# Hybrid mLSTM and sliding-window attention layer: softmax denominators through a ones column, first-head q and k kept outside the attention pool, gate rows turned later, and a front that turns x by transposes alone

## The chip, the cores and the metric

The kernel runs on one core of a Trainium2 chip. The metric is the device time of one execution in microseconds, taken as the median of the runs. Engines are named as in the profile: PE (matrix multiply), PEld (its weight loads), DVE (vector), ACT (scalar), POOL (GpSimd) and SP (the engine that issues most DMAs).

## The reference, cut to what matters

One layer on x of 1024 positions by 1024 features, all in float32:

```python
h = rms_norm(x, pre_mix_g) * (1 + sc1) + sh1          # sc1, sh1 from c @ w_ada
proj = h @ w_in                                        # q,k,v,o of 4 mLSTM heads, gates, q,k,v of attention
qk_ml = silu(causal_dwconv(qk_ml, ml_conv_w, ml_conv_b))     # 4 taps
logf = log_sigmoid(gates[..., ML_H:] + ml_f_b)
h_ml = mlstm_chunkwise(q_ml, k_ml, v_ml, i_pre, logf)  # stabilised by running maxima
...
# attention: 8 heads, 2 kv heads, window 128, blocks of 128
s = where(band, q @ k.T / 8, -inf);  m = maximum(max(s), sink)
p = exp(s - m);  denom = sum(p) + exp(sink - m);  o = (p / denom) @ v
...
x = x + g1 * rms_norm(concat(h_ml, o_at) @ w_out)
x = x + g2 * rms_norm(conv_ffn(norm(x)))               # up 1024 -> 2x2816, conv, gated gelu, down
```

## The kernel before

Every large product is a split one: each float32 operand is cut into a high and a low part (`hi`, `lo`), and `mm3` (L87) issues three matmuls for it. The work runs in stages, named here with the times at which the trace shows them.

**Front, 0 to 33 us** (it overlaps the first products). It is ordered by hand. Eight blocks of x (128 rows each) are loaded. `x_square` sums their squares on ACT, POOL makes `rst` of them, and `x_turn` (L262) turns each block so that features lie on the partitions: the first four are multiplied by `rst` on DVE (L265) and turned by eight PE transposes (L274), the last four are turned by matmuls with the diagonal matrix `dg` of `rst` (L268, L276). `x_evac` (L279) copies the turned halves to `xT` on ACT or DVE. Matmuls named `cb` spread the conditioning vector c over the partitions, and `ada_sum` (L166) multiplies it on DVE with the 48 pieces of w_ada, one 128x1024 operation each; pieces 0, 1, 8, 9 and so on are due here, the rest is spread through the later stages by `ada_bg`.

**Keys and values, 26 to 92 us**: the product for attention's k and v, then `kv_evac` (L467): rope, a copy of v to `vat` (L471), the difference `vdf` of v in this block and the one before (L473), transposes of k, and its split `khi`, `klo`. v and gates of the mLSTM heads follow.

**Attention, 112 to 236 us.** `att_group` runs twice over eight blocks of 128 queries, with four heads each (groups 0 and 1). In a block, `token_group` computes q (`tg`, L88 to L90), then `att_front` (L487) turns it, multiplies with this block's and the last block's keys (`s`, L515), and merges the two parts into one 128x128 tile per head, `sm`: the current block on and below the diagonal, the last block above it (L523, L524). DVE takes the maximum (L525) and `ngm` (L526); ACT exponentiates and sums each row (L528, `accum_out`); DVE adds the sink's term (L531) and inverts (L532). `att_back` (L535) transposes the probabilities on PE (`pt`, L538) and copies them to `pT` (L541). POOL selects the current block's part into `pN` (L545). PE multiplies (`po`, L551): pT with the last block's v, plus pN with `vdf`. DVE scales with `den` into `mix` (L554, two operations). Group 1 also squares the result on ACT (`asq`, L562). One or two ada pieces go to DVE in each block.

**Gates.** Between the two groups' code stands the chain that turns the gates of the mLSTM heads into rows (`pg`, L622 to L624), makes prefix sums and maxima of them in nearly thirty small DVE operations, stores `urow` in DRAM (`u_dram`, L657), exponentiates, and turns the results back into columns with `pg2` (L664 to L671), copied to `gcol`.

**mLSTM q and k, 186 to 340 us.** `conv_chunk` (L682) runs for q0, k0, q1, k1 to q3, k3. For each it computes the product (`cvq`, `cvk`; L88 to L90) in two halves of 512, copies them to `ub` on ACT (L692: one tile `ubq` for all q, one tile `ubk` for all k), and runs the convolution: one ACT operation and three DVE operations on a tile `cy` (L696, L698), a tanh on ACT into `z` (L699), and the product of both on DVE (L700). The tiles `cy` and `z` lie in the pool `lp`, which is opened after attention's pool `ap_` and that of the keys, `kp`, are released (L677 to L679), so the first convolution cannot start before attention's last read. `ml_head` (L703 on) loads row sums from `u_dram` into `U`, makes decay matrices `dm` on POOL and ACT (L717 to L719), weights k on DVE (`kw`, L733), and runs over eight chunks (`mS`, `st`, `tot`, L743 and around).

Then the o projection (330 to 395 us), w_out, the FFN's up product (500 to 924) and down product (924 to the end).

Except for the front, no order is written out. The framework's scheduler orders each engine's queue by its own timeline from the program's dependencies, and the number of buffers of a tile name sets when a writer waits for readers: two PSUM buffers for all of tg and cv (`mm`), and pools pA, pB, pC for s, pq/pt/xtp and po/pg.

## Time and profile before

| | us |
|---|---|
| median of 3 runs | 1156.37 (1156.13 to 1157.1) |
| the profiled execution | 1158.24 |
| its span, first to last instruction | 1156.1 |
| PE busy | 1121.0 (97%) |
| DVE busy | 859.9 (74%) |
| ACT busy | 572.0 (49%) |
| POOL busy | 189.7 (16%) |
| mean granted PE clock | 0.987 |

The profiled execution lies 1.87 us above the median; all sums are made against it and then carried over to the median. Busy time is what an engine spent in its own operations, whatever it waited for between them. A wait row names the instruction that waited, the one that released it, the total, the times and the longest wait. In a table of windows each entry is a busy time with the number of instructions in brackets, then the granted clock as a share of full speed, the share of the DMA engines and their GB/s. A timeline row gives start, duration, engine, line, output and inputs, and in square brackets the engine's idle time ahead of it and what ended that.

### The profile page before, as it was taken

The page shows a single profiled execution, that of the slowest core. Times are in us where ns is not written, and L with a number is a line of the kernel's source. Part 1 is how long each engine was busy: PE and PEld are TensorE (multiplying, and loading weights), DVE is VectorE, ACT ScalarE, POOL GpSimd, SP SyncE. Part 2 cuts the span into 40 slices and gives each one's busy share as a digit, 9 for nine tenths or more (in the row PEclk, how much of TensorE's full clock was granted, in tenths as well). Part 3 has the DMA queues.
Part 4 walks back from the last instruction along what each step waited for, and adds up shares of the span by engine and source line. Part 5 has one row for each costly group of instructions (what it writes and reads, how often), then busy time and mean ns, then how long its engine had stood idle before and what let it go on. Part 6 is the DMA issues. An engine that isn't in the chain of part 4 may idle for free.

```text
span 1156.1 us, 16247 instructions
## 1 busy us (share of the span) xinstructions
PE 1121.0 (97%) x5951; PEld 947.0 (82%) x5951; DVE 859.9 (74%) x1523; ACT 572.0 (49%) x1177; POOL 189.7 (16%) x244
## 2 busy tenths in 40 slices
PE   7999998988989999999999999999999999999997
PEld 6999997877879988877788888888888888787885
DVE  5945879478885446788897797879787874787666
ACT  6642545534444545476455454545454554345452
POOL 2022327373575400000000000000000000000021
PEclk8999998989999999999999999999999999999999
DMA  9622335151110521333332333133313468553545
GB/s 359 227 88 75 109 113 188 48 200 56 37 56 20 164 74 73 110 109 110 119 118 62 112 119 119 55 118 119 119 55 110 136 200 276 170 173 119 173 116 202
DMA packets 54464, 144.74 MB, mean 125 GB/s; under 512 B 5304, under 2 KB 5616, under 8 KB 54384
## 3 DMA queue, kind: packets, MB, share of 16 engines
q1 hardware_dynamic: 52496, 138.19, 36.0%
q10 hardware_dynamic: 1888, 5.51, 1.2%
q8 instruction: 47, 0.77, 0.3%
q14 instruction: 33, 0.27, 0.1%
HBM read 115.09 MB, written 28.60 MB: 124 GB/s over the span
## 4 chain that ended last, share of the span: by engine, by line
PE 64%; DVE 7%; POOL 3%; DMA 2%; issue 2%; ACT 2%; SPq 0%; POOLq 0%; DVEq 0%; ACTq 0%
PE X L1009 7%; PE X L1008 7%; PE X L1007 7%; PE Y L1009 4%; PE Y L1007 4%; PE Y L1008 4%; PE y L90 3%; PE y L88 3%; PE y L89 3%; DMA rb<-in_w_down_dram 2%; PE Z L1009 1%; DVE cyk L698 1%; PE Z L1007 1%; PE Z L1008 1%; PE dx L1180 1%
## 5 line engine op out<-in xcount | busy, mean ns | idle before, releaser
L93 POOL TENSOR_SCALAR rsb<-ssb 128x1 f32<-128x1 f32 x4 | 2.3, 584 | 613.0 <-ACT junk L1232 612.8
L166 DVE SCALAR_TENSOR_TENSOR ada<-ada,cb 128x1024 f32<-128x1024 f32 x48 | 61.4, 1284 | 1.5 <-DMA ada<-in_w_ada_dram 1.5
L1007 PE MATMUL X<-S,wl 128*128 128x512 f32 x156 | 62.4, 400 | 0.0
L1009 PE MATMUL X<-S,wl 128*128 128x512 f32 x156 | 61.9, 396 | 0.0
L1008 PE MATMUL X<-S,wl 128*128 128x512 f32 x156 | 61.7, 395 | 0.0
L1017 DVE SCALAR_TENSOR_TENSOR yg<-ug,cv,yg 128x1023 f32<-128x1023 f32 (+1 forms) x44 | 56.3, 1280 | 5.8 <-ACT yg L1014 5.7
L85 ACT CAST wl<-T 128x512 fp32r<-128x512 f32 x41 | 25.5, 622 | 65.5 <-PE X L1008 61.7
L1017 DVE SCALAR_TENSOR_TENSOR yv<-uv,cv,yv 128x1023 f32<-128x1023 f32 (+1 forms) x44 | 56.2, 1278 | 1.9 <-ACT yv L1014 1.9
L85 ACT CAST w<-T 128x512 fp32r<-128x512 f32 x47 | 29.1, 623 | 40.3 <-PE Z L1009 34.7
L85 DVE TENSOR_TENSOR A<-ra,A 128x512 fp32r<-128x512 f32 x46 | 31.6, 688 | 17.3 <-ACT A L85 17.2
L1061 DVE TENSOR_TENSOR uv<-q,X 128x512 f32<-128x512 f32 x22 | 15.1, 686 | 38.5 <-PE X L1009 38.5
L85 ACT CAST A<-ra 128x512 fp32r<-128x512 f32 x46 | 28.5, 620 | 30.3 <-PE dxu L1181 14.1
L85 DVE TENSOR_TENSOR w<-T,w 128x512 fp32r<-128x512 f32 x47 | 32.1, 686 | 14.8 <-ACT w L85 14.8
L85 ACT CAST B<-rb 128x512 fp32r<-128x512 f32 x44 | 27.2, 619 | 29.9 <-DMA rb<-in_w_down_dram 12.5
L85 DVE TENSOR_TENSOR B<-rb,B 128x512 fp32r<-128x512 f32 x44 | 30.2, 688 | 9.2 <-ACT B L85 8.6
L1009 PE MATMUL Y<-S,wl 128*128 128x512 f32 x92 | 36.4, 396 | 0.0
L1007 PE MATMUL Y<-S,wl 128*128 128x512 f32 x92 | 36.4, 395 | 0.0
L1008 PE MATMUL Y<-S,wl 128*128 128x512 f32 x92 | 36.2, 394 | 0.0
L85 ACT CAST wl<-fu 128x512 fp32r<-128x512 f32 x21 | 13.0, 620 | 46.7 <-PE Y L1008 43.5
L1008 PEld LDWEIGHTS X<-S,wl 128*128 128x128 f32 x156 | 29.3, 188 | 7.6 <-issue 0.5
L1007 PEld LDWEIGHTS X<-S,wl 128*128 128x128 f32 x156 | 29.3, 188 | 7.5 <-issue 0.5
L1009 PEld LDWEIGHTS X<-S,wl 128*128 128x128 f32 x156 | 29.3, 188 | 7.0
(621 smaller groups left out, 4027.6 us busy)
## 6 DMA issues: line engine op xcount, KB each, us to landing
ada<-in_w_ada_dram SPq DMA_DIRECT2D x48, 512.0 KB, 4.4
ra<-a_dram SPq DMA_DIRECT2D x30, 512.0 KB, 3.8
fu<-in_w_up_dram SPq DMA_DIRECT2D x26, 512.0 KB, 3.5
a_dram<-yg SPq DMA_DIRECT2D x22, 512.0 KB, 3.7
rb<-in_w_down_dram SPq DMA_DIRECT2D x44, 256.0 KB, 3.6
fu_False<-in_w_up_dram SPq DMA_DIRECT2D x18, 512.0 KB, 3.5
a_dram<-s SPq DMA_DIRECT2D x11, 512.0 KB, 5.1
x<-in_x_dram SPq DMA_DIRECT2D x8, 512.0 KB, 6.5
```

The lines of the kernel that those rows point to most:

```text
L85: return A.copy(hi, src), eng.tensor_tensor(lo, src, f(hi), op=ALU.subtract)
L88: T.matmul(ps, lh, rh, start=first, stop=False)
L89: T.matmul(ps, lh, rl, start=False, stop=False)
L90: T.matmul(ps, ll, rh, start=False, stop=last)
L166: return V.scalar_tensor_tensor(w, w, 0.5, cb, op0=ALU.mult, op1=ALU.mult, accum_out=mod[:, j : j + 1])
L698: V.scalar_tensor_tensor(y, ub[:, 1 + i : 1 + i + S], w(i), y, op0=ALU.mult, op1=ALU.add)
L1007: T.matmul(ps, w[:, 0, ks], a[:, 0, k, :], start=st, stop=False, skip_group_check=True)
L1008: T.matmul(ps, w[:, 0, ks], a[:, 1, k, :], start=False, stop=False, skip_group_check=True)
L1009: ends = T.matmul(ps, w[:, 1, ks], a[:, 0, k, :], start=False, stop=en, skip_group_check=True)
L1017: V.scalar_tensor_tensor(t[:, sh:], src[:, : S - sh], w(tap), t[:, sh:], op0=ALU.mult, op1=ALU.add)
L1061: V.tensor_tensor(uv[:, 512:], p5, px_, op=ALU.add)
L1180: T.matmul(ps[tb], a[:, 0, ts], w[:, 1], start=False, stop=False, skip_group_check=True)
```

## The change

**Attention.** `vat` gets a column of ones behind each kv head's 64 values, written once. `vdf` and its subtraction go. The selection on POOL is now done twice in each block but the first of a group: `pN` is the current part, and `pT` is then cut in place to the last block's part. The exponentials no longer write row sums: the 65th column of `po` holds the sum of probabilities, and `att_back` adds it to the sink's term, inverts and scales all four heads by one DVE operation.

**Pools.** `khi` and `klo` move into attention's pool. A pool `first_qk`, opened ahead of attention, holds one tile `yq`, one `yk` for heads 0 and 2 (heads 1 and 3 have theirs in `lp`). The tanh is written over `ub` and the product over `y`, so `z` and `cy` go; `ub` now stays in use until the last product has read it. Heads 1 and 3 have a `ubk` of their own for k.

**Gates.** The chain's scratch lies in the tile of `yk`. `pg` is told to come after the fourth block's product of group 1, `pg2` after the eighth's.

**Front.** All eight blocks of x are scaled on DVE and turned by transposes, the `cb` matmuls come first, and the copies of the turned halves are shared out and ordered anew.

```diff
 def x_turn(b):
-        if b < 4:
-            V.tensor_scalar(xs[b], xs[b], rst[:, b : b + 1], None, op0=ALU.mult)
-        else:
-            dg = ap0.tile([P, P], F32, tag="dg", bufs=2, name=f"dg{b}")
-            V.tensor_scalar(dg, ident, rst[:, b : b + 1], None, op0=ALU.mult)
+        V.tensor_scalar(xs[b], xs[b], rst[:, b : b + 1], None, op0=ALU.mult)
...
-                if b < 4:
-                    T.transpose(dst, src, ident)
-                else:
-                    T.matmul(dst, src, dg, start=True, stop=True)
+                T.transpose(ps[:, i * P : (i + 1) * P], xs[b][:, (4 * h + i) * P : (4 * h + i + 1) * P], ident)
...
-    vat, vdf = (ap_.tile([P, NB, P], F32, name=n) for n in ("vat", "vdf"))
+    khi = ap_.tile([P, S], F32R, name="khi")
+    klo = ap_.tile([P, S], F32R, name="klo")
+    vat = ap_.tile([P, NB, 2, 65], F32, name="vat")
+    G.memset(vat[:, :, :, 64:65], 1.0)
...
-            A.activation(sm[:, i, :], sm[:, i, :], AF.Exp, bias=ngm[:, i : i + 1], accum_out=den[:, i : i + 1])
+            A.activation(sm[:, i, :], sm[:, i, :], AF.Exp, bias=ngm[:, i : i + 1])
...
             G.affine_select(pN, pT, pattern=[[0, 4], [1, P]], compare_op=ALU.is_ge, fill=0.0, base=0, channel_multiplier=-1)
-            pTs.append((pN, vdf[:, b, :]))
+            G.affine_select(pT, pT, pattern=[[0, 4], [-1, P]], compare_op=ALU.is_ge, fill=0.0, base=-1, channel_multiplier=1)
+            pTs.insert(0, (pN, vat[:, b]))
...
+        V.tensor_tensor(den.rearrange("p (j v) -> p j v", v=2), den.rearrange("p (j v) -> p j v", v=2), po[:, :, :, 64], op=ALU.add)
+        V.reciprocal(den, den)
...
+            if gi == 1 and b == 3:
+                rows_.extend(gates_rows())
+            if gi == 1 and b == 7:
+                gates_columns(*rows_)
...
-        y = lp.tile([P, S], F32, tag="cy", bufs=1, name=f"cy{name}")
-        z = lp.tile([P, S], F32, tag=f"z{name[0]}", bufs=2, name=f"z{name}")
+        y = (yp, lp)[h % 2].tile([P, S], F32, tag=f"y{kind}", name=f"y{name}")
...
+        z = ub[:, 4 : 4 + S]
         A.activation(z, y, AF.Tanh, scale=0.5)
-        V.scalar_tensor_tensor(z, z, 1.0, y, op0=ALU.add, op1=ALU.mult)
-        return z
+        V.scalar_tensor_tensor(y, z, 1.0, y, op0=ALU.add, op1=ALU.mult)
+        return y
```

What this does to the order of the queues is seen in three places. A row of the order is a line, an operation, output and inputs (the number behind a name counts tiles) and a shape.

The first place is PE's queue where the gate rows are turned back to columns (`pg2`). Before, this stands in the middle of group 1, between its third block's output (`po1_2`) and the first matmuls of q0:

```order
L551 MATMUL po1_2_2500<-vdf_829,pN1_2_2498 128x64
L666 MATMUL pg2_2026<-ident_60,irow_1994 128x32
L666 MATMUL pg2_2026<-ident_60,crow_1997 128x32
L538 MATMUL pt1_3_2595<-ident_60,sm1_3_2352 128x128
L493 MATMUL pq1_6_2666<-ident_60,qr1_6_2658 128x128 x2
L88 MATMUL cvq0_0_2897<-hThi0_106,w10hi_2885 128x512
```

Now it stands within the second half of k0's product, next to the sixth block's output:

```order
L90 MATMUL cvk0_1_2953<-hThi1_106,w11lo_2850 128x512
L88 MATMUL cvk0_1_2953<-hThi1_106,w11hi_2849 128x512
L528 MATMUL po1_5_2757<-vat_824,pN1_5_2754 128x65
L656 MATMUL pg2_2774<-ident_60,gate_rows_1952 128x32 x3
L661 MATMUL pg2_2774<-gate_rows_1952,ones_63 128x32
L528 MATMUL po1_5_2757<-vat_824,pT1_5_2752 128x65
```

The columns moved down by some hundred and thirty rows of the queue, and what PE has queued right behind them is no longer attention's fourth block but the rest of the sixth.

The second place is DVE's queue at the convolution of q0. Before, it begins behind the last scaling of attention (`mix7`), and the ada pieces 40 to 43 lie between its steps:

```order
L554 TENSOR_TENSOR mix6_823<-po1_6_2837,den1_6_2673 128x128 x2
L554 TENSOR_TENSOR mix7_824<-po1_7_2862,den1_7_2764 128x128 x2
L698 SCALAR_TENSOR_TENSOR cyq0_2949<-ubq0_2895,cv_61,cyq0_2949 128x1024
L166 SCALAR_TENSOR_TENSOR ada40_2957,mod_65<-ada40_2957,cb_89 128x1024
L698 SCALAR_TENSOR_TENSOR cyq0_2949<-ubq0_2895,cv_61,cyq0_2949 128x1024
L166 SCALAR_TENSOR_TENSOR ada41_2960,mod_65<-ada41_2960,cb_89 128x1024
L698 SCALAR_TENSOR_TENSOR cyq0_2949<-ubq0_2895,cv_61,cyq0_2949 128x1024
L166 SCALAR_TENSOR_TENSOR ada42_3258,mod_65<-ada42_3258,cb_89 128x1024
L687 MEMSET ubq1_3196 128x4
L700 SCALAR_TENSOR_TENSOR zq0_2950<-zq0_2950,cyq0_2949 128x1024
L166 SCALAR_TENSOR_TENSOR ada43_3328,mod_65<-ada43_3328,cb_89 128x1024
```

Now its steps lie between those of attention's last block (`sm1_7`, `ngm1_7`), with no ada piece among them:

```order
L531 TENSOR_TENSOR mix4_815<-po1_4_2667,es1_4_2404 128x2x128
L692 SCALAR_TENSOR_TENSOR yq0_2907<-ubq0_2853,cv_61,yq0_2907 128x1024
L503 COPY_PREDICATED sm1_7_2714<-later_829,s1_7_0_2715 128x2x128
L503 COPY_PREDICATED sm1_7_2714<-later_829,s1_7_1_2716 128x2x128
L692 SCALAR_TENSOR_TENSOR yq0_2907<-ubq0_2853,cv_61,yq0_2907 128x1024
L504 TENSOR_REDUCE mx1_7_2712<-sm1_7_2714 128x4
L692 SCALAR_TENSOR_TENSOR yq0_2907<-ubq0_2853,cv_61,yq0_2907 128x1024
L505 SCALAR_TENSOR_TENSOR ngm1_7_2711<-mx1_7_2712,nsink_67 128x4
L508 TENSOR_TENSOR es1_7_2713<-ngm1_7_2711,rw_62 128x4
L695 SCALAR_TENSOR_TENSOR yq0_2907<-ubq0_2853,yq0_2907 128x1024
```

q0's convolution moved ahead of the scaling of three blocks and of the ada pieces 40 to 43, which now come behind k0's convolution.

The third place is ACT's queue where the second half of k1 is copied out of PSUM (`ubk`), which frees the buffer for the next product. Before, the exponentials of the first head's two decay matrices (`dm0`) stand ahead of it:

```order
L719 ACTIVATE dm0_0_3035<-dm0_0_3035 128x512
L719 ACTIVATE dm0_1_3114<-dm0_1_3114 128x512
L699 ACTIVATE zk0_3023<-cyk0_3022 128x1024
L692 COPY ubk_90<-cvk1_0_3268 128x512
L85 CAST w16hi_3564<-w16raw_3562 128x1024
L692 COPY ubk_90<-cvk1_1_3294 128x512
```

Now those of the second head stand there too, and two copies of the first head's outputs (`tot0`):

```order
L714 ACTIVATE dm0_1_3070<-dm0_1_3070 128x512
L687 COPY ubk1_3222<-cvk1_0_3224 128x512
L714 ACTIVATE dm1_0_3291<-dm1_0_3291 128x512
L745 COPY mix0_811<-tot0_0_3015 128x128
L694 ACTIVATE ubq1_3152<-yq1_3206 128x1024
L745 COPY mix1_812<-tot0_1_3025 128x128
L714 ACTIVATE dm1_1_3370<-dm1_1_3370 128x512
L85 CAST w16hi_3518<-w16raw_3516 128x1024
L687 COPY ubk1_3222<-cvk1_1_3250 128x512
```

The copy that frees k1's second PSUM buffer moved behind work of POOL for the second head and behind PE's own first outputs of the first head.

More of the change, by code (lines that the diff above doesn't have):

```diff
@@ L89, in mm3 @@
         T.matmul(ps, lh, rl, start=False, stop=False)
-        T.matmul(ps, ll, rh, start=False, stop=last)
+        return T.matmul(ps, ll, rh, start=False, stop=last)
     def rstd_of(dst, ssq, n):
@@ L302, in layer_kernel @@
     V.scalar_tensor_tensor(ch8, th8, 1.0, ch8, op0=ALU.add, op1=ALU.mult)
+    cbs = []
+    for h in range(2):
+        cbs.append((mm, pB)[h](f"cb{h}"))
+        for i in range(4):
+            k = 4 * h + i
+            T.matmul(cbs[h][:, i * P : (i + 1) * P], ident[:KD, k : k + 1].to_broadcast([KD, P]), ch8, start=True, stop=True)
     x_turn(0)
@@ L393, in ada_bg @@
             order(did, after)
+    ends = {}
     def token_group(u, n, evac):
@@ L659, in layer_kernel @@
-    frow = irow
-    wrow = crow
-    A.activation(frow, brow, AF.Exp)
-    A.activation(wrow, arow, AF.Exp, bias=urow[:, P - 1 : P])
-    A.activation(t1[:, 0:1], mprev, AF.Exp, bias=urow[:, P - 1 : P])
-    pg2 = pC("pg2")
-    for i, r in enumerate((arow, frow, wrow)):
-        T.transpose(pg2[:, 32 * i : 32 * i + 32], r, ident[:R, :R])
-    gcol = cp.tile([P, 5, 32], F32, name="gcol")
-    V.tensor_scalar(t2, ident[:R, :R], t1[:, 0:1], None, op0=ALU.mult)
-    V.tensor_scalar(t3, ident[:R, :R], mprev, None, op0=ALU.mult)
@@ new lines, in gates_columns @@
+    def gates_columns(arow, frow, wrow, t1, t2, t3, mprev):
+        pg2 = pC("pg2")
+        for i, r in enumerate((arow, frow, wrow)):
+            turned = T.transpose(pg2[:, 32 * i : 32 * i + 32], r, ident[:R, :R])
+            if i == 0:
+                order(turned, ends[8, 7])
+        V.tensor_scalar(t2, ident[:R, :R], t1[:, 0:1], None, op0=ALU.mult)
+        V.tensor_scalar(t3, ident[:R, :R], mprev, None, op0=ALU.mult)
+        T.matmul(pg2[:, 96:128], ones[:R, :], t2, start=True, stop=True)
+        T.matmul(pg2[:, 128:160], ones[:R, :], t3, start=True, stop=True)
+        V.tensor_copy(gcol, pg2[:, 0:160].rearrange("p (a b) -> p a b", a=5))
@@ L789, in layer_kernel @@
     lp.release()
+    yp.release()
     adap.release()
```

198 lines of the change are left out of this document (89 added, 109 removed).

## The prediction

> **What bounds the kernel now.** The page comes first, with the busy time of each engine.
>
> ```profile
> PE 1121.0 (97%) x5951; PEld 947.0 (82%) x5951; DVE 859.9 (74%) x1523; ACT 572.0 (49%) x1177; POOL 189.7 (16%) x244
> ```
>
> PE is busy for 1121.0 of 1156.1 us, so work taken from another engine pays only where PE stands waiting for it, or where PE works at a lower clock. The change touches nothing behind about 340 us. I therefore read next the view of waits, for PE.
>
> ```profile
> PE cvk L88 <- ACT ubq L692: 3.7, 1, 3.7
> PE cvq L88 <- ACT ubk L692: 3.2, 1, 3.2
> PE pg L666 <- ACT irow L661: 3.0, 1, 3.0
> PE st L743 <- DVE C L748: 1.8, 1, 1.8
> PE st L743 <- DVE kw L733: 1.2, 1, 1.2
> PE kv L88 <- ACT hThi L294: 0.9, 1, 0.9
> ```
>
> Three single waits stand out: 3.0 us for the gate columns, 3.7 us for the copy of q1's product, 3.2 us for that of k1's. The windows view shows what follows two of them. Its columns are PE, PEld, DVE, ACT and POOL busy, then PE's granted clock.
>
> ```profile
> 7.44:10.85 3.41, 3.40 (x16) 3.27 (x16) 2.11 (x3) 3.22 (x7) 1.85 (x5) 1.00 0.99 400
> 10.85:14.27 3.42, 3.42 (x29) 3.06 (x28) 2.24 (x4) 1.91 (x5) 1.55 (x4) 1.00 1.04 422
> 14.27:21.09 6.82, 6.23 (x30) 5.83 (x29) 2.89 (x6) 5.11 (x10) 1.47 (x4) 0.50 1.03 401
> 165.00:195.00 30.00, 27.16 (x228) 24.69 (x227) 29.56 (x84) 14.18 (x50) 17.44 (x18) 1.00 0.55 175
> 195.20:202.00 6.80, 6.80 (x22) 5.22 (x23) 6.50 (x21) 3.61 (x15) 5.18 (x6) 0.50 0.66 231
> 246.40:253.20 6.80, 5.52 (x13) 4.36 (x14) 6.77 (x8) 4.49 (x7) 6.80 (x5) 0.50 0.54 167
> ```
>
> Behind the gate wait and behind the first conv wait PE runs 6.8 us at half clock. At full clock the 6.80 us of work would take 3.4, the 5.52 would take 2.8. Together with the waits that is 3.0 + 3.4 + 3.7 + 2.8 + 3.2 = 16.1 us, all before 265 us. DVE, busy for 29.56 of 30.00 us ahead of the first wait, is the engine that PE waits for there. The timeline shows the chain at the gates.
>
> ```profile
> 194.27 0.47 DVE L658 TENSOR_TENSOR brow<-urow,brow 32x128 f32<-32x128 f32 x1
> 194.77 0.31 ACT L661 ACTIVATE irow<-brow 32x128 f32<-32x128 f32 x1 [4.97 <-DVE brow L658]
> 195.13 0.30 PE L666 MATMUL pg<-ident,irow 32*128 32x32 f32 x1 [2.97 <-ACT irow L661]
> ```
>
> And at q1, where the chain begins with attention's last read (the square on ACT), which frees the pool:
>
> ```profile
> 235.99 0.63 ACT L562 ACTIVATE asq<-mix 128x512 f32<-128x512 f32 x1 [3.55 <-DVE mix L554]
> 236.74 0.33 SPq L162 DMA_DIRECT2D ada<-in_w_ada_dram  x1
> 236.80 1.24 ACT L696 ACTIVATE cyq<-ubq,cv 128x1024 f32<-128x1024 f32 x1
> 246.09 1.06 ACT L699 ACTIVATE zq<-cyq 128x1024 f32<-128x1024 f32 x1 [1.26 <-DVE cyq L698]
> 247.06 1.05 ACT L692 COPY ubq<-cvq 128x512 f32<-128x512 f32 x2
> 247.68 0.80 PE L88 MATMUL cvk<-hThi,w13hi 128*128 128x512 f32 x1 [3.69 <-ACT ubq L692]
> ```
>
> q0's product has long been in ubq, but its convolution starts only when the pool is free, 236.80; ada pieces lie between its steps; so ubq is free at 247.06 and PE waits.
>
> **Pools and the moved q0, k0.** With `yq` and `yk` outside attention, q0's steps no longer wait for 236.7. In DVE's new queue they stand before attention's last maxima, while PE still has k0's and most of q1's products to do (over 80 matmuls, 0.23 us each by the rows below, some 20 us); so the 3.7 us wait, its 2.8 us of slow clock, and the 3.2 us wait for ubk (k1 has a tile of its own now) go. Against this, `ub` is held one tanh (1.06 us) and one DVE product longer, beside attention's tail, where two fewer head tiles are needed at once; I cost that at nothing, since two conv products (each 48 matmuls) cover it, and at some 2.3 us if the cover is gone. What is late next is k1's second copy. ACT has the exponentials of the second head's decay matrices ahead of it, and they hang on POOL:
>
> ```profile
> 243.42 1.56 POOL L717 TENSOR_TENSOR dm<-U,gcol 128x512 f32<-128x512 f32 x1 [4.99 <-DMA U<-u_dram]
> 256.46 4.51 POOL L723 TENSOR_TENSOR qw<-qw,zq 128x512 f32<-128x512 f32 x2
> 264.72 1.05 ACT L85 CAST w16hi<-w16raw 128x1024 fp32r<-128x1024 f32 x1
> 264.88 0.50 PE L88 MATMUL cvq<-hThi,w14hi 128*128 128x512 f32 x1 [3.23 <-ACT ubk L692]
> ...
> 265.46 0.39 PE L90 MATMUL cvq<-hThi,w14lo 128*128 128x512 f32 x1
> 265.69 0.39 PE L88 MATMUL cvq<-hThi,w14hi 128*128 128x512 f32 x1
> ```
>
> POOL starts the first head's `dm` 6.7 us after the pool is free (243.42 − 236.74), its chain lasts to 256.46 + 4.51 = 261.0, which is 17.5 us. With the 6.4 us of the gates gone the pool comes free near 230.3; `dm` starts near 237.0, and the chain ends near 254.5. Two `dm` and two selections of the second head follow (2 x 1.56 plus 2 x 0.64, 4.4), then an exponential (taken like a copy of 512 columns, 0.5), the cast (1.05) and two copies (1.05): 261.5. PE would be there near 264.88 − 16.1 + 1.0 (below) + 24 matmuls at 0.23 from start to start (5.6) + 23 small ones of the first head that now stand ahead, at 0.12 (29 in 3.42 us, by the window at 10.85) 2.7 = 258.1. So a wait of **3.4 us** is left; it is 0 if POOL meets less contention than the 2.25 us of each `qw` at 256.46 shows, and 2.8 more if the clock falls again as it did behind 3.7 us.
>
> **Attention.** The sums of rows leave ACT, which is not late in 165 to 195 (14.18 of 30.00). `vdf` goes. One scaling takes the place of two. The selection doubles.
>
> ```profile
> L473 DVE TENSOR_TENSOR vdf<-kv,vat x7: 281/291/292, 76.6 to 83.4; 128x128 f32<-128x128 f32 x7
> L545 POOL TENSOR_SCALAR_AFFINE_SELECT pN<-pT x14: 630/643/1649, 125.2 to 229.1; 128x512 f32<-128x512 f32 x14
> L554 DVE TENSOR_TENSOR mix<-po,den 128x128 f32<-128x128 f32 x32 | 7.8, 281 | 12.4 <-PE po L551 12.4
> 179.36 1.21 DVE L166 SCALAR_TENSOR_TENSOR ada<-ada,cb 128x1024 f32<-128x1024 f32 x1
> 179.42 1.65 POOL L545 TENSOR_SCALAR_AFFINE_SELECT pN<-pT 128x512 f32<-128x512 f32 x1
> ```
>
> `vdf` saves 7 x 0.29 = 2.0 us of DVE at 77 to 83 us, where PE does not wait for DVE: nothing. One 256-wide scaling saves between nothing and one of the two at 281 ns; at 0.1 us, nearer to nothing since as many elements are written, 16 times make 1.6 us of DVE. The second selections add 14 x 0.64 = 9.0 us of POOL at the median, 14 x 1.65 = 23.1 at the longest; the longest ran beside a DVE operation of 1.21. They lie between `pT` and `po`, behind which PE has other blocks' products: nothing on PE at the median. The additions move from in front of `po` to behind it: off PE's path, on that to `mix`. The 65th column adds one to the 64 of each `po` matmul, nothing.
>
> The Trainium skill speaks against this part: its page GPSIMD Engine Reference, section 1, Specifications, says GpSimd shares its SBUF interfaces with the vector engine and contends with DVE instructions in a 2-port mode or with two SBUF inputs. The pair of rows at 179.4 agrees.
>
> **Gates.** `pg2` stands behind the eighth block's product, so the 3.0 us and the 3.4 us of slow clock go. The chain's DVE work is the same, spread among blocks 3 to 5. What is late next is the fifth block's maximum:
>
> ```profile
> 204.38 0.17 DVE L531 TENSOR_TENSOR den<-den,es 128x4 f32<-128x4 f32 x1 [2.14 <-ACT es L530]
> 206.55 0.15 DVE L526 SCALAR_TENSOR_TENSOR ngm<-mx,nsink 128x4 f32<-128x4 f32 x1
> 212.01 0.60 PE L538 MATMUL pt<-ident,sm 128*128 128x128 f32 x4
> ```
>
> Without DVE's 2.14 us of idling for `es`, this `ngm` comes at 204.4; PE wants its transposes at 212.01 − 6.4 = 205.6, and four exponentials must fit between (1.6 us at 0.39): a wait of 0.4 us, more if the five second selections ahead of it hold DVE up (5 x (1.65 − 0.64) = 5.0). I take **1.0 us**, nearest to the median selection, from 0 to 4.
>
> **Front.** 32 diagonal products go and 32 transposes come.
>
> ```profile
> L276 PE MATMUL xtp<-dg,x 128*128 128x128 f32 x64 | 10.2, 330 | 0.7 <-ACT xT L279 0.6
> L274 PE MATMUL xtp<-ident,x 128*128 128x128 f32 x32 | 6.3, 374 | 7.4 <-DVE x L265 7.4
> L265 DVE TENSOR_SCALAR x<-x,rst 128x1024 f32<-128x1024 f32 x4 | 3.0, 749 | 1.2 <-POOL rst L94 1.2
> L268 DVE TENSOR_SCALAR dg<-ident,rst 128x128 f32<-128x128 f32 x4 | 1.1, 283 | 0.4 <-POOL rst L94 0.3
> ```
>
> The 64 matmuls took 10.2 us, as many rows as 32 float32 products need two each; 32 transposes at 6.3 save 3.9 us of PE. DVE pays 4 x (749 − 283) = 1.9 us. But the loads run at 400 GB/s and more throughout the three early windows, and the next product waits for `hThi` at 33 us (0.9 us), behind DVE's ada sums; so most of it turns into a longer wait. I take a gain of **0.3 us**, between −1.4 (first products at half clock, below) and 0.9 (that wait gone).
>
> **Sum.** 16.1 − 3.4 − 1.0 + 0.3 = 12.0 us less. The profiled execution would take 1158.24 − 12.0 = 1146.2; it lies 1.87 above the median, so the median would be 1156.37 − 12.0 = **1144.4 us**. The term bounds give 16.1 + 0.9 = 17.0 less (1139.4) to 16.1 − 6.2 − 4.0 − 1.4 = 4.5 less (1151.9).
>
> **The rivals.**
>
> *All waits go.* No new wait at the gates or k1, and earlier state products also free the `st` waits (1.8 + 1.2, with 0.9 more of smaller ones of the same kind): 16.1 + 3.9 + 0.3 = 20.3 less, 1136.1. For it: DVE is freed of ada pieces within q0. Against it: POOL is full in 246 to 253 (6.80 of 6.80), and `kw`, `C` stay where they were. Chance 0.16.
>
> *DVE and POOL become the bound.* Tail 4.0, k1 6.2 with its slow clock: 16.1 − 10.2 + 0.3 = 6.2 less, 1150.2. If pieces 40 to 47, now in one row ahead of `kw`, `sq` and q1's last product, cost another 2 to 5 us (two to four pieces at the 1.21 us above, as far as they reach PE), it is 1.2 to 4.2 less. For it: 29.56 of 30.00. Against it: DVE idles 2.14 at 204. Chance 0.22, of which 0.07 within 0.2%.
>
> *Slower: the selections lock DVE.* All 28 run at the long duration and DVE stands while they do; each second selection then costs PE 1.65 us, 23.1 in all, against 16.1 + 0.3 gained: 6.7 more, 1163.1. It decides from 16.4 / 14 = 1.17 us per selection on PE's path. For it: the pair at 179.4 us. Against it: the median is 643 ns, and PE has other blocks to work on. Chance 0.12.
>
> *The first products meet a slow clock.* The front is now transposes only. Before, the window 7.44 to 10.85, transposes alone, was followed by 1.00; the one with the small `cb` products was followed by 0.50. If transposes do not raise the clock, the first products run at half for a window of 3.4 us, lose 1.7 us, and the 0.3 us gain turns into a loss of 1.4: 10.3 less, 1146.1. Chance 0.08. The Trainium skill has this as a rule, in TensorE: Matmul & The Clock Gate, Part 4, PE-mode transpose: the full clock doesn't engage for transposes, which don't count as busy in the same way. The window row at 10.85 speaks against it, that at 14.27 for it.
>
> **How the numbers follow.** The forecast has 0.42, all gone 0.16, slow clock 0.08, DVE or POOL bound 0.22, slower 0.12. Less by over 0.2% (2.3 us, about what a measurement of this kernel can tell from no change) are 0.42 + 0.16 + 0.08 + 0.15 = 0.81; within it 0.07; slower 0.12. The range leaves out the slower case and the ends of the two outer ones: 1136.5 to 1152.5.
>
> **What would show it.** Right: no wait at `pg2`; clock 1.00 from 192 to 250; `yq` beginning before 215 us; a wait of 2 to 5 us at `cvq` for `ubk` near 258; second selections near 0.64 us. Wrong: a wait at `pt` over 2 us in 195 to 215, or DVE operations of over 2 us beside the selections (DVE bound); a wait at `po` for POOL (slower); clock 0.50 from 25 to 30 us (transposes). If the o projection starts less than 5 us earlier than before, the gain has been given back within the heads.

## The result, and the profile after

| | median us | lowest to highest | to the kernel before |
|---|---|---|---|
| before | 1156.25 | 1155.47 to 1157.1, 4 runs | |
| changed | 1148.9 | 1147.47 to 1150.41, 4 runs | ratio 0.9936, 95% interval 0.9919 to 0.9954 |

The change takes 7.4 us off (5.3 to 9.4 by the interval). The forecast was 12.0 us off, 1144.4, with a range from 1136.5 to 1152.5. The profiled execution of the changed kernel took 1150.41 us, with a span of 1148.7; it is the slowest of its four. The profiled execution of the kernel before also lay above its median, and the two spans differ by 7.5 us, close to the gain of the medians.

The page first, as before:

```profile
PE 1114.7 (97%) x5919; PEld 941.1 (82%) x5919; DVE 857.9 (75%) x1501; ACT 564.1 (49%) x1112; POOL 203.8 (18%) x259
```

PE is busy 6.3 us less (1121.0 − 1114.7), and the span is 7.4 us shorter. So only about 1 us of the gain is time in which PE stood still, where the three waits made 9.9 of the 16.1 us that I expected to go. The view of PE's waits says why (its first two rows, 6.0 and 3.8 us, are waits in the front, which had 7.4 before, and are left out):

```profile
PE st L738 <- DVE C L741: 2.5, 2, 1.4
PE tot L735 <- DVE C L743: 2.3, 2, 1.7
PE pt L515 <- ACT sm L507: 1.8, 1, 1.8
PE po L528 <- POOL pN L522: 1.7, 1, 1.7
PE dz L1175 <- ACT wl L85: 1.6, 1, 1.6
PE st L738 <- DVE kw L728: 1.2, 1, 1.2
...
PE cvq L88 <- ACT ubk L687: 0.7, 1, 0.7
```

The three waits of before are gone, all three, as the forecast said: no row for `pg`, none for `ubq`, and 0.7 us left for `ubk` where I had set 3.4. In their place stand new ones: 1.7 and 1.8 us in attention's tail, 1.4, 1.2, 1.0 and shorter ones at the state products `st` of the first heads, and 1.7 at a late `tot` (334.6 us). The kernel before had rows for `st` of much the same size (1.8 and 1.2), but those waits lay later, at 340 and 323 us. The windows, for the two stretches concerned (the first row answers to the 165 to 195 row shown for the kernel before):

```profile
165.00:195.00 30.00, 28.30 (x223) 25.08 (x222) 28.91 (x84) 15.27 (x46) 20.37 (x24) 1.00 0.61 189
195.00:215.00 20.00, 18.25 (x104) 14.69 (x103) 15.86 (x35) 11.80 (x34) 10.27 (x13) 0.83 0.27 91
236.00:262.00 26.00, 23.99 (x119) 19.50 (x118) 20.61 (x23) 7.57 (x12) 20.70 (x14) 1.00 0.67 220
262.00:280.00 18.00, 15.53 (x90) 12.34 (x89) 15.08 (x32) 10.07 (x26) 9.21 (x11) 1.00 0.08 30
```

PE's idle time in the last two rows is 2.0 + 2.5 us, in a stretch where the convolutions were to be out of the way. The timeline shows the three places, each a queue in which something longer stands ahead. In attention's tail, POOL's weight split `w12lo` stands ahead of the selection for which PE waits, and `ngm`, made from the maxima, runs 2.24 us beside the split `w13lo`, ending 0.02 us behind it:

```profile
189.85 2.39 POOL L85 TENSOR_TENSOR w12lo<-w12raw,w12hi 128x1024 fp32r<-128x1024 f32 x1
...
193.99 0.63 POOL L522 TENSOR_SCALAR_AFFINE_SELECT pN<-pT 128x512 f32<-128x512 f32 x1
```
```profile
207.05 2.24 DVE L505 SCALAR_TENSOR_TENSOR ngm<-mx,nsink 128x4 f32<-128x4 f32 x1
```
```profile
206.90 2.37 POOL L85 TENSOR_TENSOR w13lo<-w13raw,w13hi 128x1024 fp32r<-128x1024 f32 x1
```

In the heads, DVE idles for the DMA of an ada piece (its tile lies in the pool that opens behind attention) and then has several pieces and a step of q1's convolution ahead of the first state `C`:

```profile
238.79 1.23 DVE L164 SCALAR_TENSOR_TENSOR ada<-ada,cb 128x1024 f32<-128x1024 f32 x1 [3.51 <-DMA ada<-in_w_ada_dram]
...
252.26 2.30 DVE L164 SCALAR_TENSOR_TENSOR ada<-ada,cb 128x1024 f32<-128x1024 f32 x1
...
254.50 0.28 DVE L741 COPY C<-st 128x129 f32<-128x129 f32 x1
```
```profile
254.84 0.38 PE L738 MATMUL st<-mix,kw 128*128 128x129 f32 x1 [1.41 <-DVE C L741]
```

To see where the rest came from I took, from each trace, the stretch from PE's first matmul of attention's q (first `tg` with w6) to its first of the up product (`e`), and sorted the time from each matmul's start to the next: over 0.15 us above the kind's usual pace is a wait, what is more than the pace inside a window of half clock is clock, the rest is pace (an estimate of mine from the records, good to some tenths).

| stretch q to up product, us | length | waits | slow clock | pace, above the usual |
|---|---|---|---|---|
| before | 396.9 | 17.8 | 5.3 | 3.5 |
| changed | 391.5 | 16.8 | 4.1 | 0.3 |

The rest of the 7.4 us lies ahead of that stretch (0.5) and behind it (1.5, by a shorter wait at `dz` in the down product and no half clock behind it this time). Of the 5.4 us, 3.2 is pace: matmuls standing in a better order. Most of it, 2.8, sits in attention's products `s`, which are the same 192 matmuls:

```profile
L515 PE MATMUL s<-khi,qhi 64*128 64x256 f32 (+1 forms) x64 | 12.9, 326 | 0.0
L515 PE MATMUL s<-klo,qhi 64*128 64x256 f32 (+1 forms) x64 | 10.9, 279 | 0.0
L515 PE MATMUL s<-khi,qlo 64*128 64x256 f32 (+1 forms) x64 | 10.8, 287 | 0.0
```
```profile
L494 PE MATMUL s<-khi,qhi 64*128 64x256 f32 (+1 forms) x64 | 11.0, 326 | 0.0
L494 PE MATMUL s<-khi,qlo 64*128 64x256 f32 (+1 forms) x64 | 9.7, 281 | 0.0
L494 PE MATMUL s<-klo,qhi 64*128 64x256 f32 (+1 forms) x64 | 9.7, 276 | 0.0
```

The first fence is the kernel before, the second the changed one. The busy times of these groups overlap each other; summed from each matmul's start to the next one's, the 192 take 17.9 us before and 15.1 now. Two such matmuls, of the two kv heads, use 64 rows of the array each, and when two stand next to each other the second can start within 0.04 us of the first. By the traces 78 of the 192 start that close in the kernel before and 91 in the changed one, and most other neighbours start about 0.11 behind. The matmuls of other kinds also break them up less, into 19 rows instead of 24.

### The profile page after: what moved, and what is told of

It is laid out like the page before. It is cut to its first block, busy times and chain, and to the rows that moved or that the text cites. A ratio compares the mean times of both kernels' runs of the same rounds, so it can differ in the third digit from the quotient of the medians.

```text
span 1148.7 us, 16112 instructions
## 1 busy us (share of the span) xinstructions
PE 1114.7 (97%) x5919; PEld 941.1 (82%) x5919; DVE 857.9 (75%) x1501; ACT 564.1 (49%) x1112; POOL 203.8 (18%) x259
## 4 chain that ended last, share of the span: by engine, by line
PE 78%; DVE 12%; DMA 4%; ACT 2%; issue 2%; POOL 1%; SPq 1%; DVEq 0%; POOLq 0%; ACTq 0%
PE X L1005 7%; PE X L1004 7%; PE X L1003 7%; PE Y L1005 4%; PE Y L1003 4%; PE Y L1004 4%; DVE ada L164 3%; PE tg L88 3%; PE y L88 3%; PE y L90 3%; PE y L89 3%; PE tg L89 3%; PE tg L90 3%; DMA rb<-in_w_down_dram 2%; PE Z L1005 1%
## 5 line engine op out<-in xcount | busy, mean ns | idle before, releaser
L164 DVE SCALAR_TENSOR_TENSOR ada<-ada,cb 128x1024 f32<-128x1024 f32 x48 | 64.5, 1351 | 7.4 <-DMA ada<-in_w_ada_dram 7.2
L85 ACT CAST w<-T 128x512 fp32r<-128x512 f32 x47 | 29.1, 623 | 40.7 <-PE Z L1005 34.7
L1057 DVE TENSOR_TENSOR uv<-q,X 128x512 f32<-128x512 f32 x22 | 15.1, 686 | 38.4 <-PE X L1005 38.4
L85 DVE TENSOR_TENSOR A<-ra,A 128x512 fp32r<-128x512 f32 x46 | 31.7, 689 | 15.9 <-ACT A L85 15.4
```

What stands on the lines that cost most here:

```text
L85: return A.copy(hi, src), eng.tensor_tensor(lo, src, f(hi), op=ALU.subtract)
L164: return V.scalar_tensor_tensor(w, w, 0.5, cb, op0=ALU.mult, op1=ALU.mult, accum_out=mod[:, j : j + 1])
L1057: V.tensor_tensor(uv[:, 512:], p5, px_, op=ALU.add)
```

## The experiments

The first theory was that the pools carry the gain, that the late gates carry little, and that DVE's crowded ada pieces give part of it back. The rival: the gain comes from elsewhere, and what the pools save is lost within the heads. All ratios are to the kernel before, run on the same chip within the same minutes.

| run | what it is | median us | ratio | 95% interval |
|---|---|---|---|---|
| e7 | changed, once more | 1148.75 | 0.9926 | 0.9907 to 0.9945 |
| e1 | changed, old front | 1147.68 | 0.9924 | 0.9903 to 0.9945 |
| e2 | changed, old pools | 1150.48 | 0.9943 | 0.9923 to 0.9963 |
| e5 | changed, gates early | 1149.09 | 0.9938 | 0.9917 to 0.9959 |
| e4 | changed, ada late | 1142.64 | 0.9879 | 0.9856 to 0.9902 |
| e3 | changed, no second selection | 1153.33 | 0.9968 | 0.9956 to 0.9981 |
| e8 | changed, ada late, gates early | 1141.8 | 0.9867 | 0.9846 to 0.9888 |
| e6 | before + attention | 1145.05 | 0.9891 | 0.9871 to 0.9911 |
| e12 | before + late gates | 1153.64 | 0.9967 | 0.9949 to 0.9985 |
| e10 | before + attention + late gates | 1149.19 | 0.9927 | 0.9902 to 0.9951 |
| e11 | before + attention + pools | 1148.15 | 0.9920 | 0.9901 to 0.9939 |
| e9 | before + attention, ada late | 1143.69 | 0.9884 | 0.9866 to 0.9902 |

**Taking back one part: front (e1), pools (e2), gates (e5).**

```diff
# e1: x_turn and the order of the front as before
...
# e2: pools and conv_chunk as before
-    yp = tc.alloc_tile_pool(name="first_qk", bufs=1, side="right")
+    kp = tc.alloc_tile_pool(name="keys", bufs=1, side="right")
...
# e5: between the two groups, and without the two order() calls
+    gates_columns(*gates_rows())
     ensure(10)
     att_group(8, 1)
```

> The changed kernel with the front of before (four blocks scaled and transposed, four turned by diagonal products, cb matmuls in their old place). Theory: the new front is worth next to nothing, since the first k, v products end 0.5 us earlier in the changed kernel's trace (the last at 73.61 against 74.09): this kernel takes 1149.4 us, within 1 us of the changed kernel's 1148.9. Rival: the 6.8 us at half clock that the transposes leave behind cost their full price, 3.4 us of products, and the front is a loss: 1146 to 1147.

> The changed kernel with the pools of before: keys outside attention, q0's and k0's convolution in the pool that opens behind it, z and cy apart, one ubk for all k. Theory: the pools carry the gain, since the two waits at 243 and 261 us (3.7 and 3.2) and 2.8 us of slow clock come back: 1148.9 + 6 to 9 = 1155 to 1158. Rival: what they save is given back inside the heads, where the state products now wait 4 to 6 us for DVE, and the gain is that of the other parts: 1149 to 1152.

> The changed kernel with the gate rows and columns where they stood in the program of before, between the groups, without the order that holds pg and pg2 back. Theory: the wait at pg2 comes back with its slow clock (3.0 + 3.4), less the two waits that took its place in 190 to 210 (1.7 and 1.8 with 1.7 of slow clock each): about the same, 1148 to 1151. Rival: the late gates are the gain: 1154 to 1156.

Measured: 1147.68, 1150.48 and 1149.09. The intervals of all three hold the changed kernel's own ratio. The front is worth nothing that can be measured; e1's median lies between the theory (within 1 us of 1148.9) and the rival (1146 to 1147), and its interval does not tell them apart. The pools were expected to cost 6 to 9 us when taken back; beside the repeat they cost some 2 us (0.9943 against 0.9926), which the intervals do not tell from nothing: the rival holds. The two waits do come back in e2's trace, with 8.0 us together where the kernel before had 6.9, and yet the time hardly moves:

```profile
PE cvq L88 <- ACT ubk L684: 5.7, 1, 5.7
...
PE cvk L88 <- ACT ubq L684: 2.3, 1, 2.3
```

And with the gates early (e5) no wait at the gate columns comes back at all. So that wait had been removed by something other than the late gates. e5's time fits the theory, but its reason, that wait coming back, is not what happened. Its trace has the stretch from q to the up product 3.8 us shorter than the changed kernel's (387.7 against 391.5) and loses 0.9 ahead of it and 2.7 behind it, where the wait at `dz` is 2.0 instead of 1.6 and one of 2.0 stands at `dx`.

**The attention part alone (e6).**

```diff
 # the kernel before, with the attention hunks of the change
-            A.activation(sm[:, i, :], sm[:, i, :], AF.Exp, bias=ngm[:, i : i + 1], accum_out=den[:, i : i + 1])
+            A.activation(sm[:, i, :], sm[:, i, :], AF.Exp, bias=ngm[:, i : i + 1])
...
```

> The kernel before with the attention part of the change alone: ones column, no row sums by ACT, no vdf, two selections in each block, one scaling. Theory, after the runs that took back one part each and lost little: this part alone removes the wait at the gate columns with its slow clock (6.4 us), since the sums, inversions and vdf no longer stand in DVE's queue ahead of the gate chain and the maxima, and it brings the s products of the two kv heads next to each other in PE's queue (2.8 us less for the same 192 matmuls); the waits at the convolutions stay: 1156.4 - 6 to 9 = 1147 to 1150. Rival: it removes nothing alone, since the chain of the gates stands where it stood: 1155 to 1157, or slower by the selections: 1158 and more.

Measured: 1145.05, 0.9891. This is 2 us below the range expected. This part alone gives as much as the whole change and likely more: beside the repeat of the change on the same chip (0.9926) it is 3.7 us faster, with intervals that just touch. Its view of PE's waits still has the convolutions' two waits, at 5.0 and 4.0 us, and no row for the gate columns:

```profile
PE cvk L88 <- ACT ubq L688: 5.0, 1, 5.0
PE cvq L88 <- ACT ubk L688: 4.0, 1, 4.0
```

Its timeline has the chain of the gates 8 to 13 us earlier than before (194.27 and 195.13 there), and PE does not wait:

```profile
180.85 0.44 DVE L654 TENSOR_TENSOR brow<-urow,brow 32x128 f32<-32x128 f32 x1
```
```profile
186.52 0.25 PE L662 MATMUL pg<-ident,irow 32*128 32x32 f32 x1
```

The stretch from q to the up product takes 385.4 us: waits 12.4, slow clock 3.3, pace −0.7. Of the 11.5 us against before, about 5.4 are waits, 2.0 clock and 4.2 pace. Of the pace, 2.8 is again `s` (17.9 to 15.1 from start to start). The groups of instructions show what the edit takes away. Before, ACT spent 24.9 us in exponentials and 12.0 in reading sums, and DVE stood 13.0 us at the additions `den`, waiting for ACT:

```profile
L528 ACT ACTIVATE sm<-sm,ngm 128x128 f32<-128x128 f32 x64 | 24.9, 390 | 11.1 <-DVE ngm L526 9.8 <-DVE mod L176 1.3
L528 ACT ACTIVATION_READ_ACCUMULATOR sm<-sm,ngm 128x1 f32 x64 | 12.0, 188 | 0.0
```
```profile
L531 DVE TENSOR_TENSOR den<-den,es 128x4 f32<-128x4 f32 x16 | 5.4, 335 | 13.1 <-ACT es L530 13.0
```

With the attention part:

```profile
L526 ACT ACTIVATE sm<-sm,ngm 128x128 f32<-128x128 f32 x64 | 20.5, 391 | 23.4 <-DVE ngm L524 23.3
```
```profile
L548 DVE TENSOR_TENSOR es<-es,po 128x4 f32<-128x4 f32 x16 | 2.4, 152 | 14.1 <-PE po L547 14.1
```

By the timelines ACT is through with a block's four exponentials in 1.28 us where it took 1.62 (194.99 to 196.61). DVE's 14.1 us for `po` take the place of the 12.4 that it stood for `po` at the old scalings, so by these rows the 13.0 for `es` are what it no longer waits.

How the gate chain came to be earlier is another matter, for most of those 13.0 us lie behind it, at 204 to 224 us. The windows from PE's first matmul of attention's q to the end of the chain's `brow` (the kernel before, then e6), and the additions within the first:

```profile
98.32:194.74 96.42, 93.84 (x792) 87.44 (x790) 81.89 (x241) 44.65 (x162) 39.12 (x52) 1.00 0.41 127
99.95:181.29 81.34, 81.34 (x727) 77.36 (x726) 70.46 (x211) 35.05 (x107) 34.66 (x51) 1.00 0.42 130
```
```profile
L531 DVE TENSOR_TENSOR den<-den,es 128x4 f32<-128x4 f32 x11 | 3.7, 338 | 3.3 <-ACT es L530 3.2
```

Counted from q, which starts 1.6 us later in e6, the chain is through 15.1 us sooner. DVE has 11.4 us less work ahead of it (81.89 against 70.46) and stands idle 3.7 us less. Of the work, by the timelines, 3.4 are three ada pieces that now stand behind the chain, and 1.8 the scalings (one block fewer among them). Another 3.8 are two small operations in DVE's queue just ahead of the chain's end. In the kernel before each ran beside a weight split on POOL and ended with it; the like take 0.15 and 0.46 in e6:

```profile
186.12 2.39 POOL L85 TENSOR_TENSOR w11lo<-w11raw,w11hi 128x1024 fp32r<-128x1024 f32 x1
186.50 2.03 DVE L531 TENSOR_TENSOR den<-den,es 128x4 f32<-128x4 f32 x1
189.07 2.36 POOL L85 TENSOR_TENSOR w12lo<-w12raw,w12hi 128x1024 fp32r<-128x1024 f32 x1
189.10 2.36 DVE L669 TENSOR_SCALAR gt<-ident,mcol 32x32 f32<-32x32 f32 x1
```

PE's wait at the gate columns was 3.0 us, less than these two cost. So part of the gain is work that the edit takes away, and part only where the scheduler put pieces and splits. Which of the sub-edits (row sums off ACT, the sum's place in DVE's queue, no `vdf`, one scaling) does how much was not separated.

**The selections (e3).** The kernel leaves out the second selection, a part of the computation.

```diff
-            G.affine_select(pT, pT, pattern=[[0, 4], [-1, P]], compare_op=ALU.is_ge, fill=0.0, base=-1, channel_multiplier=1)
```

> The changed kernel without the second selection, so that pT keeps both blocks' probabilities (part of the computation left out). If the 14 second selections cost PE what the slower rival says, 1.65 us each, 23 us go: 1126. Theory: they run beside other blocks' products at 0.64 us and cost nothing but part of the waits for pN and for sm at 192 and 207 us (3.5 us with 3 of slow clock): 1143 to 1148.

Measured: 1153.33, 4.6 us slower than with them. Both expectations miss. In its trace POOL has `w11lo` ahead of one `pN`, PE waits 3.90 us there, and 10.2 us of half clock lie around it (the stretch: waits 16.3, clock 7.5):

```profile
187.49 2.33 POOL L85 TENSOR_TENSOR w11lo<-w11raw,w11hi 128x1024 fp32r<-128x1024 f32 x1
189.79 0.64 POOL L522 TENSOR_SCALAR_AFFINE_SELECT pN<-pT 128x512 f32<-128x512 f32 x1
```
```profile
190.49 0.69 PE L527 MATMUL po<-vat,pN 128*128 128x65 f32 x2 [3.90 <-POOL pN L522]
```

So leaving the second selections out gave no gain that can be seen; PE waits for POOL longest where the scheduler has put a 2.3 us weight split ahead of a first selection. That wait and the half clock behind it do not explain the whole: e3's waits sum to no more than the changed kernel's (16.3 against 16.8), and 4.2 of them are a wait for ACT's squares (`jk`) at 272 us. The run also says how far any of these runs can be trusted: leaving work out moved the time up, with the queues laid out anew.

**Ada late (e4), and with the gates early (e8).**

```diff
-        V.scalar_tensor_tensor(y, z, 1.0, y, op0=ALU.add, op1=ALU.mult)
+        ends[name] = V.scalar_tensor_tensor(y, z, 1.0, y, op0=ALU.add, op1=ALU.mult)
...
-        for _ in range((2, 1, 1, 1)[h]):
-            ada_bg(lp)
+        for _ in range((0, 0, 2, 2)[h]):
+            ada_bg(lp, ends[f"q{h}"])
# the same behind k; e8 has the edit of e5 too
```

> The changed kernel with the ada pieces 40 to 47 taken from the stretch of the first two heads' convolutions (two behind the last product of each of q2, k2, q3, k3 instead). Theory: DVE's pieces, crowded at 245 to 264 us since they all wait for attention's pool, hold back the state products (waits of 2.5, 1.2 and 0.7 us for C and kw): 3 to 6 us less, 1143 to 1146. Rival: the state chain and POOL bound that stretch and the pieces lie in DVE's idle time: 1148 to 1150.

> The changed kernel with the ada pieces 40 to 47 late, as in the run that took 1142.6 us, and the gate rows and columns at their old place in the program. Theory: in 190 to 215 the two waits (1.9 and 1.9) and the two stretches of slow clock that the late rows bring go too, 4 to 6 us: 1137 to 1139. Rival: what is won there is lost behind the last head, where the gates-early kernel waited 3.1 us: 1141 to 1143.

Measured: 1142.64 for e4, 6 us under the changed kernel, with an interval clear of the changed kernel's repeat. The theory holds here (0.4 us below its range), and the windows of e4 show it: in 236 to 262 us DVE is down from 20.61 to 10.80 us of work, and PE is busy for all of it.

```profile
236.00:262.00 26.00, 26.00 (x138) 21.85 (x138) 10.80 (x16) 12.05 (x24) 18.58 (x15) 1.00 0.31 98
262.00:280.00 18.00, 17.32 (x96) 14.72 (x95) 14.19 (x24) 6.75 (x18) 10.23 (x11) 1.00 0.19 58
```

e8 took 1141.8, the fastest of all kernels here, but the interval overlaps e4's; its expected 1137 to 1139 missed, and the rival's 1141 to 1143 holds, but not by the rival's reason. The waits around 190 to 215 fall from 3.4 to 0.8 us and both stretches of half clock there go; the stretch from q to the up product is 4.1 us shorter than e4's (381.9 against 386.1), as the theory said. In these two profiles it is given back outside that stretch: 0.6 ahead of it and 3.2 behind it, where e8 waits 1.8 us at `dz` (e4 1.0) and has half clock from 979.2 to 982.6. One profile of each does not tell whether that comes with the kernel or with the execution.

**Adding parts to attention (e10, e11), late gates by themselves (e12).**

```diff
# e10: before + attention + the gates_rows()/gates_columns() hunks
# e11: before + attention + pools and conv_chunk of the change, the gates' scratch in the tile of yk
# e12: before + the gates_rows()/gates_columns() hunks, scratch in attention's pool
```

> The kernel before with two parts of the change, attention and the late gates (old front, old pools). The attention part alone took 1145.05 us. Theory: the late gates cost, since the chain's DVE operations move from 162 to 190 us into the stretch of blocks 3 to 5, where the maxima then wait behind them: 4 to 6 us more than attention alone, 1149 to 1151. Rival: they are free and the loss from 1145 to 1148.8 belongs to pools and front: 1144 to 1146.

> The kernel before with attention and pools (old front, gates early). Theory: the waits at the convolutions (5.0 and 4.0 with 3.3 of slow clock in the attention-only trace) go, but ada pieces crowded ahead of the state products and waits at the last head take most of it: 1143 to 1147, no more than 2 us from attention alone. Rival: the 12 us go in full and only the late gates gave them back: 1133 to 1138.

> The kernel before with the late gates alone. By the forecast's step the wait at pg2 and its slow clock (6.4 us) go and about 1 us comes back: 1151. Theory: DVE is the engine that is late in that stretch and the chain only moves within it, so the waits come back at the maxima of blocks 4 and 5: 1154 to 1158.

Measured: 1149.19, 1148.15 and 1153.64. On top of attention the late gates cost about 4 us (0.9927 against 0.9891), the pools about 3 (0.9920); the intervals overlap at their edges, so each by itself is likely, not certain. e11 is 1 us above the range expected. Alone, on the kernel before, the late gates gain some 4 us (4.5 by the medians), between the forecast's step and the theory. In the stretch from q to the up product:

| us | length | waits | clock | pace |
|---|---|---|---|---|
| before | 396.9 | 17.8 | 5.3 | 3.5 |
| before + late gates | 393.1 | 16.7 | 3.4 | 2.8 |
| before + attention | 385.4 | 12.4 | 3.3 | −0.7 |
| ... + late gates | 389.7 | 16.2 | 3.5 | −0.4 |
| ... + pools | 389.0 | 14.3 | 4.8 | −0.4 |
| ... + all (the change) | 391.5 | 16.8 | 4.1 | 0.3 |
| change, ada late and gates early | 381.9 | 10.3 | 1.4 | −0.2 |

The table leaves out what lies ahead of the stretch and behind it, where the profiles differ by up to 4 us, so its lengths do not add up to the medians. Three pairs agree on the late gates once attention is changed: they lengthen the stretch by 3.8 us (the change against e5), 4.3 (e10 against e6) and 4.1 (e4 against e8). The pools have no such constant price: on attention alone they lengthen it by 3.7 (e11), and with the late gates they shorten it by 2.1 (e2 has 393.6).

With attention in place the gate chain is early enough by itself. Holding it back brings it into the stretch where the blocks' maxima are due, and the changed kernel's waits for `pN` and for `sm` appear in e10:

```profile
PE pt L537 <- ACT sm L529: 1.7, 1, 1.7
PE po L550 <- POOL pN L544: 1.7, 1, 1.7
```

**Ada late with the old pools (e9).** The same edit as e4 on e6.

> The kernel before with attention and with the ada pieces 40 to 47 late (behind the last product of q2, k2, q3, k3), old pools, gates and front. Theory: the pieces between the steps of q0's and k0's convolutions are the larger part of the waits for ubq and ubk (5.0 and 4.0), so without moving the convolutions out of the pool the time falls by 4 to 8 us: 1137 to 1141. Rival: the release of attention's pool sets these waits, pieces or not: 1144 to 1146.

Measured: 1143.69, 0.9884, no different from e6's 1145.05. It fits the rival (1144 to 1146) better than the theory (1137 to 1141). One of the two waits stays and one goes:

```profile
PE cvk L88 <- ACT ubq L690: 4.6, 1, 4.6
PE tot L736 <- ACT jk L751: 2.4, 3, 1.2
```

So the wait for `ubq` (4.6, before 3.7) is set by the pool, the one for `ubk` by the ada pieces; much of what the second gave came back at the later heads (`jk` 2.4 against 0.5 in e6, and 1.3 for DVE's `mden`). Over attention alone the pools by themselves lost 3 us, the late pieces by themselves gained under 1, and both together (e8, which has the new front too) gained 2.8; the intervals of all three overlap that of attention alone.

## Why the prediction was right, and where it was wrong

It was right in the sign and within its range, but by a sum whose parts were mostly wrong: a gain that it put at nothing (the attention part) and losses that it did not have (late gates, pools with crowded ada pieces) happened to leave nearly what its waits would have. That the number came within the range is in good part luck. Its total was 4.6 us too large.

**Right:** the waits at the gate columns and for `ubq` go, the one for `ubk` falls from 3.2 to 0.7, and the slow clock at 246 goes. The front is worth nothing that can be measured; what `vdf` and the 65th column are worth by themselves no run shows. `yq` begins at 210.6, before 215 as said. The second selections run at their faster duration (629/634/1622 ns as shortest, median and longest), and the case in which they cost 1.65 us each on PE's path did not come.

**Signs that spoke against it:** the clock is not 1.00 from 192 to 250, k1's wait is not 2 to 5 us, and the o projection starts only 2.6 us earlier (327.8 against 330.4), under the 5 us that the prediction named as the mark of a gain given back within the heads.

**The step that failed first: "off PE's path".** The forecast costed the attention part at nothing on PE: sums leave ACT, "which is not late in 165 to 195", additions move, "off PE's path". Alone it measured 12 us less (0.9891; 10 to 15 by the interval). The mistake was to ask of each edit whether PE waits for that engine now, and not what else stands behind the instruction in its queue. PE's wait at the gate columns was the end of DVE's queue: with the attention part DVE has 11.4 us less work and 3.7 us less idling ahead of the end of the gate chain, and the wait is gone. Only 3.2 of the 13.0 us that DVE stood for `es` lie ahead of the chain; two small operations held back by weight splits on POOL are 3.8 of the work. How much of it is the edit and how much the new order stays open. I put the wait down to the gates' place in the program and credited it to the gates' edit.

**The second: the 16.1 us of waits, added up.** Waits of one stretch were summed as if each would vanish alone. With attention in place the gates' 6.4 us had gone already, and holding the gates back had only its cost left. The term for the tail, 1.0 us, was mis-sized: two waits of 1.7 and 1.8 us and two windows of half clock (3.4 each, at 196.3 and 210.0), as much half clock as the 6.8 us at 195 that were to go. Neither lies at the maximum that I priced: I called it the fifth block's, by its row at 206.55 it is the sixth's, and in the changed kernel it comes at 201.7 and PE does not wait for it. One wait is for the selection at 193.99 behind `w12lo`, the other for the seventh block's maximum, and there it was not a selection but a weight split that held DVE: 2.24 us of `ngm` beside `w13lo`.

**The third: k1's wait, 3.4 us, against 0.7.** POOL's chain was about as long as expected but began 4.7 us later (its first `dm` at 241.65, where I had 237.0; its second head's `dm` and selections end at 263.0, where I had 258.9), and PE came later too, at 264.5 and not 258.1, having waited for `C` and `kw`. These waits, 5.6 us in 250 to 292 by the records, were not in the sum; they stood in the rival "DVE and POOL become the bound", with pieces 40 to 47 in a row ahead of `kw` and `sq` named as its mechanism. That part of the rival is shown by e4: take the pieces away and 6 us go. Its 1150.2 was nearer to 1148.9 than the forecast.

**The fourth, not seen at all:** PE's own pace, 3.2 us of it, 2.8 in `s`. The pairs of `s` matmuls could have been counted in the new order before the result; only places where PE waits had been looked at.

**The slow clock of the transposes.** In the changed kernel's trace the first products do run at half clock, from 24.95 to 28.9 us, which the prediction had named as the sign of that rival. The front's rows on PE:

```profile
6.04 3.78 PE L297 MATMUL cb<-ch,ident 8*128 8x128 f32 x16 [6.04 <-DVE ch L291]
9.74 6.50 PE L265 MATMUL xtp<-ident,x 128*128 128x128 f32 x32
16.73 1.06 PE L265 MATMUL xtp<-ident,x 128*128 128x128 f32 x8 [0.49 <-DVE x L261]
```

The transposes start 0.21 us apart up to 15.4 us and 0.11 apart from there on: the clock rose after 5.7 us of nothing but transposes, with the `cb` matmuls ahead of them. In the kernel before, PE's first work is 3.4 us of transposes alone, and the next window is at full pace (29 instructions against 16, in the prediction's rows). The Trainium skill's rule in TensorE: Matmul & The Clock Gate, Part 4, PE-mode transpose, that the full clock doesn't engage for them, is not borne out here. The traces do not show in which mode of PE the program's `transpose` calls run. The half clock from 22.3 to 29.1 begins between two gaps, of 1.5 and 1.7 us, in which PE waited for x. And it changes from run to run: the repeat (e7) has it from 24.9 to 28.3, e8 with the same front not until 33.7, the old front from 14.3 to 21.1 in before and not at all in e1. The front's price, e1 against e7, is nothing that can be measured (0.9924 against 0.9926).

## What to carry to other kernels

Where an engine that works in order is full, look at all that stands in its queue ahead of the instruction that PE waits for, work and idling both: an edit that takes some of it away may remove a wait whose name is another's. Waits of one stretch are not a sum: price each edit again with the others already made, and suspect that the second and third cure of one wait have only their costs left. When a scheduler lays the queues out, even an edit that only leaves work out can move the time by 4 or 5 us, as e3 did; measure parts alone and together before crediting one.

The version to keep is the change with the ada pieces 40 to 47 late: 1142.64, or 1141.8 with the gates early as well. By the intervals the much smaller edit, attention alone (1145.05) or with the late pieces (1143.69), is not told apart from either.

## What the runs showed of the hardware

Two matmuls of 64 rows each, of the two kv heads, can start within 0.04 us of each other when they are neighbours in the queue; most other neighbours among them start about 0.11 us apart. With 91 instead of 78 such close starts among the 192, in 19 rows instead of 24, the time from start to start fell from 17.9 to 15.1 us.

Small DVE operations on 128x4 elements whose two inputs both lie in SBUF took 0.15 us alone; when they began during a GpSimd subtraction of 128x1024 they ended 0.02 us behind it, however early they had begun: `ngm` (207.05 to 209.29) beside `w13lo` (206.90 to 209.27), and in the kernel before `ngm` at 136.78 (2.11 us) beside `w10lo`. The ones in the changed kernel that do not have two such inputs ran through: the addition of `po`, which lies in PSUM, to `es` took 0.16 us at 227.83 and the reciprocal 0.18 at 228.03, both inside `w14lo` (226.78 to 229.13).
